# Tail and second half of an attention layer: denominators by transposes, a third weight buffer, residuals loaded ahead, other filler portions

## The chip, the cores and the metric

The kernel runs on one core of one Trainium2 chip, in one launch. The metric is the device time of an execution in microseconds, and the lower it is the better. The engines are TensorE (PE: matrix products and transposes), VectorE (DVE), ScalarE (ACT) and GpSimd (POOL). SyncE (SP) issues nearly all the DMA transfers, in one queue, in order.

## The reference

Two trunk layers over 1024 tokens of width 1024, with 256 context tokens ahead of them. Layer 0 is a mix of chunked gating and Fourier mixing; the change leaves it alone. Layer 1 is windowed attention with 16 query heads, 4 key/value heads of width 64, 256 context keys, a window of 128 to either side, a sink logit for each head and a SiLU gate, then an output product, a gated residual and the final RMS norm over channels:

```
q, k, v, g = split_c(h @ w_in)
...
p = sink_softmax(jnp.concatenate([s_ctx, s_win], axis=-1), sink_b)
...
y = (o * jax.nn.silu(g)) @ w_out_c[i]
...
x = x + gate * y
return rms_norm(x, final_g)
```

So a value after attention is `o` divided by its softmax denominator, times `silu(g)`; that product, called y below, is what the last weight matrix multiplies.

## The kernel before

**Precision and tiles.** Activations stand transposed, channels on partitions and tokens in the free dimension. Every large product is done as three products of split operands: an operand is cast to a short format (hi, by ACT), the rest is subtracted (lo, by POOL or DVE), and hi·hi, lo·hi and hi·lo are accumulated (L108, L109, L110). A 128x1024 weight block comes by DMA into one of three raw buffers (`w_dma`), becomes `wh` on ACT and `wl` on POOL (`w_split`), and serves a tile of 128 output channels. y is split in pieces of 128 channels, k = 0 to 7 (`y_split` puts them in a queue, `pop_y` does one, `need_y` does what a product is about to read).

**The attention.** `attention` runs 32 units: 8 blocks n of 128 queries, with 4 key/value groups j each. `period` is a table of times for one unit u and the next unit v, written by hand and sorted: the score products S of v in two halves (PE, L1626 and L1627), `ttr` (mask and running maximum, DVE, L1644), `exp` (ACT, L1652), transposes T of the probabilities (PE, L1674, into the PSUM tile pt with two buffers), their splits `ph` (ACT) and `pl` (DVE), the products with V of u (PV), and `oev`/`oadd`, which bring the result into `osum`. S of the second half overwrites the scores that `ttr` reads, so it waits for DVE. PE, DVE, ACT and POOL run what the program says in that order; in SP's queue a scheduler has placed the transfers.

**The filler.** Between these steps `F` gives PE other work in portions of PE time, `NF` us for each period: first the products for the gates g and the last q of later blocks (`gen_q`, `gen_g`), then the output product (`gen_out`). That one needs y of the first 512 tokens (c = 0) and so starts in period `SPLIT`, at its tenth us; c = 1 covers tokens 512 to 767. `gen_out` loads the residual `xr` of a tile when it starts it, and its evacuation (DVE, L1492) adds it.

**The denominators.** For a block, `block_a` writes the reciprocals `rinv` to DRAM as `rd`, `block_r` reads them back spread over partitions as `rb`, `block_m` multiplies them with G (`silu(g)`) on POOL and `block_b` multiplies by `osum`. For blocks 0 to 6 that is done once for all 16 heads; for block 7 after each of its 4 units, with 4 heads each.

**The tail.** `tail` does the last 256 tokens in 8 tiles, in the order 6, 7, 0 to 5, with two more pairs of weight buffers (`whx`, `wlx`), and beside it the generator `final` norms what is finished: a column sum on PE, a root on ACT, a reciprocal, a diagonal matrix `t` of it (DVE, L1322), its spread by PE (S<-t,ones, L1329) and the scaled output `ot`. These lines are those that the change alters:

```
def w_dma(self):
    while len(self.raws) < 2 and self.wsrc:
...
if self.raws and len(self.wready) < (2 if self.WT else 1) and (self.WT or self.wn < 31):
...
NF = (4.95, 4.8)
SPLIT = 18
```

## Time and profile before

| | us |
|---|---|
| median of 3 runs | 1116.36 (1116.27 to 1117.07) |
| the profiled execution | 1113.16 |
| its span, first to last instruction | 1111.4 |
| PE busy in it | 1042.1 (94%) |
| DVE, ACT, POOL busy | 660.0, 511.9, 456.2 |
| mean granted clock of PE | 0.977 |

The profiled execution is 3.2 us shorter than the median of the timed runs, and its span is 1.8 us shorter than itself. PE is busy nearly all the time, so what is of interest are the stretches in which it isn't, and those in which its granted clock is below 1.00. The attention starts at 654 us, unit by unit, with a period of 11.7 to 12.3 us where there is filler. Its last product ends at 1052.6 us, the last tile of the tail at 1100.8 us.

### The profile page before, as it was taken

Reading aid. Unit: us, or ns where it says so; the run is one execution under the profiler, and the core shown is the slowest. Engines: PE = TensorE matmul, PEld = TensorE weight load, DVE = VectorE, ACT = ScalarE, POOL = GpSimd, SP = SyncE. Lnnn points to the kernel's source line nnn. Section 1 sums busy time; section 2 is a strip of 40 time slices with the busy share of each in tenths; the row PEclk is TensorE's granted clock in tenths of the full one; section 3 lists DMA queues with packets and bytes.
Section 4 is the critical chain, followed back from the end, with each engine's and each line's share of the span. In section 5 each row is a group of like instructions: output and inputs, shape, how many; then the busy total and the mean of one; then the engine's idle time right before and its main releaser. Section 6 shows DMA issues by size and latency. Waiting matters only on the chain. (4 is left out here: it accounts for less than half of the span.)

```text
span 1111.4 us, 15531 instructions
## 1 busy us (share of the span) xinstructions
PE 1042.1 (94%) x5682; PEld 882.9 (79%) x5682; DVE 660.0 (59%) x1266; ACT 511.9 (46%) x1006; POOL 456.2 (41%) x295
## 2 busy tenths in 40 slices
PE   9889999999999999998989989999999799997885
PEld 7668888887888888886779878888888678886784
DVE  7982666676774545339653006777666767665444
ACT  4463232232122343324232336677666766676642
POOL 2633322253321373547732434666131352436642
PEclk9989999999999999999999999999999999999987
DMA  9720322352124464424421243848242443434344
GB/s 339 269 96 13 120 87 84 109 169 95 57 76 136 148 210 150 140 89 128 146 87 39 95 128 123 131 146 153 58 133 55 109 113 96 99 88 110 105 134 161
DMA packets 102849, 133.94 MB, mean 121 GB/s; under 512 B 24050, under 2 KB 70386, under 8 KB 102772
## 3 DMA queue, kind: packets, MB, share of 16 engines
q1 hardware_dynamic: 101476, 129.13, 39.5%
q0 software_dynamic: 1296, 3.81, 1.1%
q8 instruction: 45, 0.74, 0.3%
q14 instruction: 32, 0.26, 0.1%
HBM read 116.46 MB, written 16.84 MB: 120 GB/s over the span
## 5 line engine op out<-in xcount | busy, mean ns | idle before, releaser
L103 POOL TENSOR_TENSOR wl<-raw,wh 128x1024 fp32r<-128x1024 f32 x80 | 197.9, 2475 | 338.2 <-ACT wh L98 338.2
L110 PE MATMUL mm<-hh,wl 128*128 128x512 f32 (+1 forms) x592 | 215.5, 364 | 3.9 <-POOL wl L103 3.9
L108 PE MATMUL mm<-hh,wh 128*128 128x512 f32 (+1 forms) x592 | 216.8, 366 | 1.4 <-ACT wh L98 1.3
L109 PE MATMUL mm<-hl,wh 128*128 128x512 f32 (+1 forms) x592 | 215.1, 363 | 0.0
L1644 DVE CUSTOM_DVE_ANT_0 P<-S,mask,nsink 128x640 f32<-128x640 f32 (+1 forms) x128 | 103.9, 847 | 90.1 <-PE S L1627 90.1
L1683 DVE TENSOR_TENSOR pl<-pt,ph 128x512 fp32r<-128x512 f32 x152 | 104.0, 689 | 73.1 <-ACT ph L1679 71.3
L110 PEld LDWEIGHTS mm<-hh,wl 128*128 128x128 f32 x592 | 112.1, 189 | 24.2 <-POOL wl L103 4.8
L1679 ACT CAST ph<-pt 128x512 fp32r<-128x512 f32 x152 | 88.4, 584 | 88.1 <-PE pt L1674 87.5
L108 PEld LDWEIGHTS mm<-hh,wh 128*128 128x128 f32 x592 | 112.3, 190 | 20.6 <-ACT wh L98 2.2
L109 PEld LDWEIGHTS mm<-hl,wh 128*128 128x128 f32 x592 | 112.5, 190 | 18.4
L1652 ACT ACTIVATE P<-P,m 128x640 f32<-128x640 f32 (+1 forms) x128 | 101.9, 800 | 7.7 <-DVE m L1644 7.7
L348 DVE CUSTOM_DVE_ANT_0 junk<-raw,cb 128x1024 bf16<-128x1024 f32 x56 | 84.0, 1501 | 27.9 <-DMA raw<-in_ada_wT_dram 27.5
L98 ACT CAST wh<-raw 128x1024 fp32r<-128x1024 f32 x80 | 83.3, 1043 | 28.5 <-PE mm L109 8.9
L1674 PE MATMUL pt<-ident,P 128*128 128x128 f32 x608 | 92.9, 274 | 2.7 <-DVE pl L1683 1.7
L1674 PEld LDWEIGHTS pt<-ident,P 128*128 128x128 f32 x608 | 75.8, 141 | 23.8 <-DVE pl L1683 2.5
L1626 PE MATMUL S<-kk,qh 128*128 128x256 f32 (+1 forms) x256 | 75.0, 310 | 7.4 <-DVE m L1644 5.2
L1627 PE MATMUL S<-kk,ql 128*128 128x256 f32 (+1 forms) x256 | 71.4, 304 | 0.7 <-DMA ql<-qd 0.7
L110 PE MATMUL mm<-rh,hl 128*128 128x512 f32 x160 | 64.3, 402 | 4.5 <-POOL hl L472 4.5
L108 PE MATMUL mm<-rh,hh 128*128 128x512 f32 x160 | 64.8, 405 | 3.6 <-ACT hh L470 3.6
L1691 PE MATMUL O<-ph,V 128*128 128x512 f32 x152 | 63.9, 420 | 1.2 <-DVE osum L1707 0.9
L109 PE MATMUL mm<-rl,hh 128*128 128x512 f32 x160 | 63.4, 396 | 0.0
L1692 PE MATMUL O<-pl,V 128*128 128x512 f32 x152 | 60.8, 400 | 0.3 <-DVE pl L1683 0.3
(270 smaller groups left out, 2203.6 us busy)
## 6 DMA issues: line engine op xcount, KB each, us to landing
raw<-in_w2i_dram SPq DMA_DIRECT2D x34, 512.0 KB, 3.5
raw<-in_ada_wT_dram SPq DMA_DIRECT2D x32, 512.0 KB, 3.5
raw<-in_w2o_dram SPq DMA_DIRECT2D x22, 512.0 KB, 4.0
raw<-in_w1o_dram SPq DMA_DIRECT2D x16, 512.0 KB, 3.5
qh<-qd SPq DMA_DIRECT2D x64, 128.0 KB, 3.9
ql<-qd SPq DMA_DIRECT2D x64, 128.0 KB, 3.7
raw<-in_w1i_dram SPq DMA_DIRECT2D x12, 512.0 KB, 4.7
qd<-t SPq DMA_DIRECT2D x24, 256.0 KB, 4.5
```

The lines of the kernel that those rows point to most:

```text
L98: nc.scalar.copy(out=hi, in_=src)
L103: (nc.vector if lo_eng == "dve" else nc.gpsimd).tensor_tensor(out=lo, in0=src, in1=f32(hi), op=ALU.subtract)
L108: mm(ps, lhsT=lhi, rhs=rhi, start=first, stop=False)
L109: mm(ps, lhsT=lhi, rhs=rlo, start=False, stop=False)
L110: mm(ps, lhsT=llo, rhs=rhi, start=False, stop=last)
L348: nc.vector.tensor_tensor_reduce(out=junk, in0=raw, in1=self.cb[:, i, :], scale=1.0, scalar=0.0, op0=ALU.mult, op1=ALU.add, accum_out=cols ...
L1626: nc.tensor.matmul(S[:, o_:o_ + nn], lhsT=self.qh[:, hs], rhs=kk[:, t0:t0 + nn], start=True, stop=False)
L1644: nc.vector.tensor_tensor_reduce(out=self.P[pr][:, e, :T], in0=k.S[:, so:so + T], in1=k.mask[:, m], scale=-1.0, scalar=k.nsink[:, h:h + 1] ...
L1652: self.K.nc.scalar.activation(out=P, in_=P, func=AF.Exp, bias=self.m[:, h:h + 1], scale=-1.0, accum_out=self.m[:, 16 + h:17 + h])
L1674: nc.tensor.transpose(pt[:, h * 128:(h + 1) * 128], self.P[h // 2][:, h % 2, co:co + 128], k.ident)
L1679: k.nc.scalar.copy(out=self.hl[ci][0], in_=self.pt[ci])
L1683: self.K.nc.vector.tensor_tensor(out=lo, in0=self.pt.pop(ci), in1=f32(hi), op=ALU.subtract)
```

## The change

- `w_dma` of the attention's first weights stands behind the first two units' q loads in the program.
- `NF` is 4.45 and then 4.5, and in the blocks 0 and 7 1.3 more; `SPLIT` is 17.
- `w_split` may run two weights ahead in the attention too, with a third pair of buffers (`wh3`, `wl3`, for every third weight).
- The lo part of y of k = 1, 4 and 7 goes to DVE (in the last 256 tokens, k = 6 and 7 as before).
- `xr` is loaded a tile ahead (`xr_next`), through to the end of the tail.
- Blocks 0 to 6: `block_r` is at 10.0 of the period rather than 2.0, `block_m` at 5.0 rather than 3.0, `block_b` at 8.0 rather than 7.5.
- Block 7: the way through DRAM is gone. `block_t` transposes each head's `rinv`, spread over 128 columns, on PE into a pt buffer, and two DVE instructions multiply G by it; `block_b` multiplies by `osum`.
- Tail: the queued pieces of y go ahead of the first weight split, which the second follows behind the load of ACT's root table; 8 buffers `ot` rather than 4; `t` is made by ACT, but for the last; two more steps lie between it and its use.

```diff
-        self.w_dma()
         for u in U[:2]:
             u.load()
+        self.w_dma()
...
-            nf = self.NF[i >= self.SPLIT]
+            nf = self.NF[i >= self.SPLIT] + (1.3 if u.n in (0, 7) else 0)
...
-    NF = (4.95, 4.8)
-    SPLIT = 18
+    NF = (4.45, 4.5)
+    SPLIT = 17
...
-        for _ in range(2):
-            self.w_split()
+        while self.sq2:
+            self.pop_y()
+        self.w_split()
         dum = self.t(self.const, [128, 1], F32, "dum")
         nc.scalar.activation(out=dum, in_=self.eps, func=AF.Sqrt)
+        self.w_split()
...
-            xr = self.t(self.OP, [128, 512], F32, "xr", 2)
-            nc.sync.dma_start(out=xr[:, hs], in_=self.x1d[:, j, 768:1024])
+            xr = self.xr.pop(0)
+            self.xr_next()
...
-            nc.vector.tensor_scalar(out=dg[:, b * 128:b * 128 + 128], in0=self.ident, scalar1=r[:, b:b + 1],
-                                    scalar2=None, op0=ALU.mult)
-        yield 1
-        yield 1
+            if last:
+                nc.vector.tensor_scalar(out=dg[:, b * 128:b * 128 + 128], in0=self.ident, scalar1=r[:, b:b + 1],
+                                        scalar2=None, op0=ALU.mult)
+            else:
+                nc.scalar.mul(out=dg[:, b * 128:b * 128 + 128], in_=self.ident, mul=r[:, b:b + 1])
+        for _ in range(4):
+            yield 1
...
-                ot = self.t(self.WT, [128, 512], F32, "ot", 4)
+                ot = self.t(self.WT, [128, 512], F32, "ot", 8)
...
-        if self.raws and len(self.wready) < (2 if self.WT else 1) and (self.WT or self.wn < 31):
+        if self.raws and len(self.wready) < 2 and (self.WT or self.wn < 31):
...
-            pool, tg = (self.WT, "x") if self.wn >= 31 else (self.WS, "")
+            pool, tg, nb = (self.WT, "x", 2) if self.wn >= 31 else (self.AT, "3", 1) if self.wn % 3 == 1 else (self.WS, "", 2)
...
-                    lo_eng="dve" if c and hs.start and k > 5 else "pool")))
+                    lo_eng="dve" if (k > 5 if hs.start else k % 3 == 1) else "pool")))
...
+    def xr_next(self):
+        if self.xrl:
+            j, o, hs = self.xrl.pop(0)
+            xr = self.t(self.OP, [128, 512], F32, "xr", 2)
+            self.nc.sync.dma_start(out=xr[:, hs], in_=self.x1d[:, j, o + hs.start:o + hs.stop])
+            self.xr.append(xr)
...
-                at(10.8, self.block_a, v.n, v.j)
+                if v.n < 7:
+                    at(10.8, self.block_a, v.n)
         if u.n == 7 or u.j == 3:
-            at(2.0, self.block_r, u.n, u.j)
+            at(*(1.95, self.block_t, u.j) if u.n == 7 else (10.0, self.block_r, u.n))
         if u.n == 7:
-            at(8.0, self.block_m, u.n, u.j)
             at(10.95, self.block_b, u.n, u.j)
         if prev and prev.n < 7 and prev.j == 3:
-            at(3.0, self.block_m, prev.n, prev.j)
-            at(7.5, self.block_b, prev.n, prev.j)
+            at(5.0, self.block_m, prev.n)
+            at(8.0, self.block_b, prev.n, prev.j)
...
+    def block_t(self, j):
 
         nc = self.nc
...
+        p = self.t(self.ps, [128, 512], F32, "pt", 2)
+        for h in range(4):
+            nc.tensor.transpose(p[:, h * 128:h * 128 + 128], self.bl[7][0][:, 4 * j + h:4 * j + h + 1].broadcast_to([128, 128]), self.ident)
         for e in range(2):
...
+            g = self.G[64 * e:64 * e + 64, 2 * j:2 * j + 2, 896:1024]
+            nc.vector.tensor_tensor(out=g, in0=p[64 * e:64 * e + 64].rearrange("p (i e q) -> p e i q", i=2, e=2)[:, e], in1=g, op=ALU.mult)
```

**Where the order moves.** SP's queue, in before, from the write of block 6's reciprocals (rd6) through that of the first unit of block 7 (rd7); qh and ql are q loads of units to come, raw a weight block:

```order
L1572 DMA rd6_681_4138<-rinv_1459_8363 128x16x1 [waits DMAHW0_49,DVE_49]
L1474 DMA xr_1606_9005<-x1d_537_3179 128x256 [waits DMAHW1_49,DVE_49]
L1584 DMA rb_1579_8903<-rd6_681_4138 64x8x128 [waits DMAHW2_49,DMAHW0_49]
L1584 DMA rb_1579_8903<-rd6_681_4138 64x8x128 [waits DMAHW3_49]
L1382 DMA raw0_1613_9034<-in_w2o_dram 128x1024 [waits DMAHW4_49,Pool_49]
L1617 DMA qh_1616_9043<-qd_674_4131 64x4x128 [waits DMAHW5_49,PE_49]
L1617 DMA qh_1616_9043<-qd_674_4131 64x4x128 [waits DMAHW6_49]
L1617 DMA ql_1617_9044<-qd_674_4131 64x4x128 [waits DMAHW7_49,PE_49]
L1617 DMA ql_1617_9044<-qd_674_4131 64x4x128
L1572 DMA rd7_682_4139<-rinv_1572_8885 128x4x1 [waits DMAHW1_49,DVE_49]
L1474 DMA xr_1627_9124<-x1d_537_3179 128x256 [waits DMAHW2_49,DVE_49]
L1584 DMA rb7_1619_9054<-rd7_682_4139 64x2x128 [waits DMAHW3_49,DMAHW1_49]
```

SP's queue in the changed kernel, from the same write on:

```order
L1584 DMA rd6_681_4138<-rinv_1469_8399 128x16x1 [waits DMAHW2_49,DVE_49]
L1471 DMA xr_1553_8809<-x1d_537_3179 128x256 [waits DMAHW3_49,DVE_49]
L1590 DMA rb_1610_9017<-rd6_681_4138 64x8x128 [waits DMAHW4_49,DMAHW2_49]
L1590 DMA rb_1610_9017<-rd6_681_4138 64x8x128 [waits DMAHW5_49]
L1635 DMA qh_1620_9073<-qd_674_4131 64x4x128 [waits DMAHW6_49,PE_49]
L1635 DMA qh_1620_9073<-qd_674_4131 64x4x128 [waits DMAHW7_49]
L1635 DMA ql_1621_9074<-qd_674_4131 64x4x128 [waits DMAHW0_49,PE_49]
L1635 DMA ql_1621_9074<-qd_674_4131 64x4x128 [waits DMAHW1_49]
L1471 DMA xr_1603_8983<-x1d_537_3179 128x256 [waits DVE_49]
L1387 DMA raw2_1634_9155<-in_w2o_dram 128x1024 [waits DMAHW3_49,Pool_49]
L1635 DMA qh_1650_9247<-qd_674_4131 64x4x128 [waits DMAHW4_49,PE_49]
L1635 DMA qh_1650_9247<-qd_674_4131 64x4x128 [waits DMAHW5_49]
```

The read rb of block 6 still stands directly behind its write and the residual, and q loads behind it; the writes and reads of block 7 are gone, and a weight block and the next residual stand in their place.

POOL in before, from the start of c = 1 (oacc is the sum of squares, wl a weight's lo part, yl a piece of y):

```order
L1500 TENSOR_TENSOR oacc0_1312_7702<-oacc0_1312_7702,t_1567_8873 128x512 [waits Activation_49,Pool_49]
L103 TENSOR_TENSOR wl_1569_8877<-raw0_1513_8618,wh_1568_8876 128x1024 [waits DMAHW6_49,PE_49,Activation_49]
L103 TENSOR_TENSOR yl0_1562_8851<-G_759_4580,yh0_1561_8850 128x256 [waits Activation_49]
L103 TENSOR_TENSOR yl1_1564_8856<-G_759_4580,yh1_1563_8855 128x256 [waits PE_49,Activation_49]
L1500 TENSOR_TENSOR oacc0_1312_7702<-oacc0_1312_7702,t_1610_9027 128x512 [waits Activation_49,Pool_49]
L103 TENSOR_TENSOR wl_1612_9031<-raw1_1539_8744,wh_1611_9030 128x1024 [waits DMAHW5_49,PE_49,Activation_49]
L103 TENSOR_TENSOR yl2_1581_8910<-G_759_4580,yh2_1580_8909 128x256 [waits Activation_49]
L103 TENSOR_TENSOR yl3_1587_8939<-G_759_4580,yh3_1586_8938 128x256 [waits Activation_49]
L1589 TENSOR_TENSOR rb_1579_8903<-rb_1579_8903,G_759_4580 128x1024 [waits DMAHW3_49,DMAHW2_49]
```

POOL in the changed kernel, at the same place:

```order
L103 TENSOR_TENSOR wl_1560_8826<-raw1_1497_8523,wh_1559_8825 128x1024 [waits DMAHW4_49,PE_49,Activation_49]
L103 TENSOR_TENSOR yl0_1556_8816<-G_759_4580,yh0_1555_8815 128x256 [waits PE_49,Activation_49]
L1515 TENSOR_TENSOR oacc0_1295_7616<-oacc0_1295_7616,t_1580_8904 128x512 [waits Activation_49,Pool_49]
L103 TENSOR_TENSOR yl2_1567_8848<-G_759_4580,yh2_1566_8847 128x256 [waits PE_49,Activation_49]
L103 TENSOR_TENSOR yl3_1575_8882<-G_759_4580,yh3_1574_8881 128x256 [waits PE_49,Activation_49]
L103 TENSOR_TENSOR yl5_1590_8932<-G_759_4580,yh5_1589_8931 128x256 [waits PE_49,Activation_49]
L1515 TENSOR_TENSOR oacc0_1295_7616<-oacc0_1295_7616,t_1614_9057 128x512 [waits Activation_49,Pool_49]
L103 TENSOR_TENSOR wl3_1616_9061<-raw2_1533_8705,wh3_1615_9060 128x1024 [waits DMAHW2_49,PE_49,Activation_49]
L103 TENSOR_TENSOR yl6_1596_8961<-G_759_4580,yh6_1595_8960 128x256 [waits Activation_49]
L1595 TENSOR_TENSOR rb_1610_9017<-rb_1610_9017,G_759_4580 128x1024 [waits DMAHW5_49,DMAHW4_49]
```

The last oacc of c = 0 and a weight's lo part still stand together ahead of a piece of y: of yl2 before, of yl6 now, with yl1 and yl4 not on POOL any more.

DVE in before, from the second norm of the tail to the evacuation of the last tile (L1305):

```order
L1287 TENSOR_TENSOR oacc1_1313_7703<-pt_1755_9884,oacc1_1313_7703 128x256 [waits Activation_49]
L1319 RECIPROCAL rl512_1759_9901<-rl512_1759_9901 128x2 [waits Activation_49]
L1322 TENSOR_SCALAR t_1760_9910<-ident_5_100,rl512_1759_9901 128x128 [waits DVE_49,Pool_49]
L1322 TENSOR_SCALAR t_1760_9910<-ident_5_100,rl512_1759_9901 128x128
L1280 SCALAR_TENSOR_TENSOR G_759_4580<-mm_1754_9876,gth_838_5357,xr_1753_9874 128x256 [waits DMAHW4_49,PE_49]
L1287 TENSOR_TENSOR oacc1_1313_7703<-pt_1763_9929,oacc1_1313_7703 128x256 [waits Activation_49]
L1347 TENSOR_TENSOR ot512_1764_9941<-G_759_4580,S_1713_9645 128x256 [waits PE_49]
L1347 TENSOR_TENSOR ot512_1764_9941<-G_759_4580,S_1713_9645 128x256 x2
L1280 SCALAR_TENSOR_TENSOR G_759_4580<-mm_1762_9921,gth_838_5357,xr_1761_9919 128x256 [waits DMAHW0_49,PE_49]
L1287 TENSOR_TENSOR oacc1_1313_7703<-pt_1767_9968,oacc1_1313_7703 128x256 [waits Activation_49]
L1347 TENSOR_TENSOR ot512_1764_9941<-G_759_4580,S_1713_9645 128x256 x5
L1305 SCALAR_TENSOR_TENSOR G_759_4580<-mm_1766_9960,gth_838_5357,xr_1765_9958 128x256 [waits DMAHW1_49,PE_49]
```

DVE in the changed kernel, to the evacuation of the last tile (L1307) and beyond:

```order
L1282 SCALAR_TENSOR_TENSOR G_759_4580<-mm_1757_9886,gth_838_5357,xr_1747_9836 128x256 [waits DMAHW6_49,PE_49,Pool_49]
L1289 TENSOR_TENSOR oacc1_1296_7617<-pt_1766_9938,oacc1_1296_7617 128x256 [waits Activation_49]
L1321 RECIPROCAL rl512_1763_9926<-rl512_1763_9926 128x2
L1282 SCALAR_TENSOR_TENSOR G_759_4580<-mm_1765_9930,gth_838_5357,xr_1756_9884 128x256 [waits DMAHW3_49,PE_49,Pool_49]
L1289 TENSOR_TENSOR oacc1_1296_7617<-pt_1769_9972,oacc1_1296_7617 128x256 [waits Activation_49]
L1352 TENSOR_TENSOR ot512_1770_9984<-G_759_4580,S_1717_9658 128x256 [waits PE_49]
L1352 TENSOR_TENSOR ot512_1770_9984<-G_759_4580,S_1717_9658 128x256 x7
L1307 SCALAR_TENSOR_TENSOR G_759_4580<-mm_1768_9964,gth_838_5357,xr_1764_9928 128x256 [waits DMAHW5_49,PE_49,Pool_49]
L1311 TENSOR_SCALAR G_759_4580<-G_759_4580,fg_673_4129 128x256 [waits Activation_49]
```

The diagonal t of the second norm is not on DVE any more, and all eight outputs ot512 now stand in one piece directly ahead of the evacuation of the last tile, where three of them stood a tile earlier.

## Rows read from the trace of the kernel before

**Rows 1.** Waits of TensorE's (PE) instructions, 650 to 665 us: total us, times, longest.
```profile
PE S L1626 <- DMA qh<-qd: 2.1, 1, 2.1
PE S L1627 <- DMA ql<-qd: 0.7, 1, 0.7
```

**Rows 2.** Stretches, without and with filler: us, busy us per engine (instructions), PEclk, DMA, GB/s.
```profile
860.00:892.00 32.00, 25.87 (x149) 20.34 (x148) 24.22 (x48) 23.89 (x54) 10.98 (x7) 1.00 0.42 109
904.00:1000.00 96.00, 96.00 (x544) 81.34 (x545) 65.37 (x136) 66.14 (x142) 35.36 (x19) 1.00 0.44 112
```

**Rows 3.** Waits of PE's instructions, 785 to 905 us.
```profile
PE S L1626 <- DVE m L1644: 4.0, 7, 1.1
```

**Rows 4.** Waits of PE's instructions, 997 to 1035 us.
```profile
PE mm L110 <- POOL wl L103: 3.4, 2, 1.9
PE mm L109 <- POOL yl L103: 3.1, 2, 2.6
```

**Rows 5.** Waits of PE's instructions, 1035 to 1065 us.
```profile
PE mm L108 <- DVE G L1492: 4.1, 3, 3.1
```

**Rows 6.** Waits of PE's instructions, 1065 us to the end.
```profile
PE S L1329 <- DVE t L1322: 4.3, 2, 3.4
PE mm L109 <- DVE yl L103: 1.9, 1, 1.9
PE mm L108 <- DVE G L1280: 1.4, 1, 1.4
PE mm L108 <- ACT yh L98: 1.0, 1, 1.0
```

**Rows 7.** Stretches from 997.5 us on, columns as in rows 2.
```profile
997.50:1010.00 12.50, 9.45 (x54) 8.25 (x53) 6.25 (x14) 7.23 (x17) 8.94 (x8) 0.86 0.57 138
1022.50:1035.00 12.50, 10.58 (x70) 9.92 (x70) 5.95 (x17) 7.96 (x19) 5.57 (x6) 0.86 0.39 105
1047.50:1060.00 12.50, 9.40 (x64) 8.85 (x63) 2.79 (x6) 4.80 (x10) 6.81 (x6) 0.90 0.26 64
1060.00:1072.50 12.50, 9.36 (x67) 8.75 (x66) 5.02 (x7) 6.80 (x13) 7.84 (x7) 0.91 0.53 180
1072.50:1085.00 12.50, 12.07 (x93) 11.85 (x93) 6.92 (x16) 5.74 (x9) 5.14 (x3) 0.92 0.39 123
1085.00:1097.50 12.50, 7.71 (x45) 7.33 (x44) 7.08 (x13) 2.88 (x6) 4.41 (x2) 0.77 0.52 180
```

**Rows 8.** Chain that ended last, in order of time: start us, us, what.
```profile
996.29 0.23 PE mm L108
...
997.68 0.44 PE pt L1674 x4
...
1044.32 11.63 DMA rd<-rinv
...
1081.11 4.54 DMA out_dram<-ot
```

**Rows 9.** Waits of SP's DMA queue, whole span.
```profile
SPq L1584 <- DMA rd<-rinv: 103.2, 11, 10.4
```

**Rows 10.** Groups on DVE, POOL, ACT, 1000 us on: xcount | busy, mean ns | idle before.
```profile
L1707 DVE TENSOR_TENSOR osum<-O,osum 64x256 f32<-64x256 f32 x10 | 4.2, 417 | 0.1
L1595 DVE TENSOR_TENSOR G<-rb,osum 128x256 f32<-128x256 f32 x4 | 2.9, 714 | 4.1 <-POOL rb L1589 4.0
L1322 DVE TENSOR_SCALAR t<-ident,rl 128x128 f32<-128x128 f32 x8 | 3.6, 501 | 0.2
L1347 DVE TENSOR_TENSOR ot<-G,S 128x256 f32<-128x256 f32 x14 | 4.9, 412 | 1.0 <-ACT rlast L1332 1.0
...
L103 POOL TENSOR_TENSOR wlx<-raw,whx 128x1024 fp32r<-128x1024 f32 x6 | 14.2, 2381 | 14.5 <-ACT whx L98 14.5
...
L98 ACT CAST whx<-raw 128x1024 fp32r<-128x1024 f32 x6 | 6.2, 1041 | 4.9 <-PE mm L109 4.9
```

**Rows 11.** One tile, yl: its DVE instructions, ns min/median/max.
```profile
L103 DVE TENSOR_TENSOR yl<-G,yh x2: 413/1336/2260, 1067.1 to 1069.3; 128x256 fp32r<-128x256 f32 x2
```

More of the change, by code (lines that the diff above doesn't have):

```diff
@@ L1461, in need_y @@
             self.pop_y()
+    def xr_next(self):
[4 more added lines that the diff above has]
+            self.xr.append(xr)
     def gen_out(self):
         self.wkeep = {}
+        self.xrl = [(j, 512 * c, slice(0, 256 if c else 512)) for c in range(2) for j in range(8)]
+        self.xrl += [(j, 512, slice(256, 512)) for j in (6, 7, 0, 1, 2, 3, 4, 5)]
+        self.xr = []
+        self.xr_next()
         for c in range(2):
@@ L1472, in gen_out @@
                     self.wkeep[j] = w
-                xr = self.t(self.OP, [128, 512], F32, "xr", 2)
-                self.nc.sync.dma_start(out=xr[:, hs], in_=self.x1d[:, j, o:o + n])
+                xr = self.xr.pop(0)
+                self.xr_next()
                 p = self.t(self.ps, [128, 512], F32, "mm", self.MMB)
@@ L1565, in period, with block_a @@
         return ev
-    def block_a(self, n, j):
-        nc = self.nc
-        j0, nj = (j, 1) if n == 7 else (0, 4)
-        rinv = self.bl[n][0]
-        nc.sync.dma_start(out=self.rd[n][4 * j0:4 * (j0 + nj)].rearrange("h q -> q h"), in_=rinv[:, 4 * j0:4 * (j0 + nj)],
-                          allow_slow_non_contiguous=True)
-    def block_r(self, n, j):
-        nc = self.nc
-        j0, nj = (j, 1) if n == 7 else (0, 4)
-        if j0 == 0:
-            self.rbs[n] = self.t(self.AT, [128, 8, 128], F32, "rb7" if n == 7 else "rb", 1)
-        rv = self.rd[n].rearrange("(i e) q -> e i q", e=2)
-        s = slice(2 * j0, 2 * (j0 + nj))
-        rb = self.rbs[n][:, s, :]
+    def block_a(self, n):
+        self.nc.sync.dma_start(out=self.rd[n].rearrange("h q -> q h"), in_=self.bl[n][0], allow_slow_non_contiguous=True)
@@ new lines, in block_r, with block_m @@
+    def block_r(self, n):
+        rb = self.rbs[n] = self.t(self.AT, [128, 8, 128], F32, "rb", 1)
+        rv = self.rd[n].rearrange("(i e) q -> e i q", e=2)
+        for e in range(2):
+            self.nc.sync.dma_start(out=rb[64 * e:64 * e + 64], in_=rv[e:e + 1].broadcast_to([64, 8, 128]))
+    def block_m(self, n):
+        rb = self.rbs[n]
+        self.nc.gpsimd.tensor_tensor(out=rb, in0=rb, in1=self.G[:, :, n * 128:(n + 1) * 128], op=ALU.mult)
+    def block_t(self, j):
+        nc = self.nc
+        p = self.t(self.ps, [128, 512], F32, "pt", 2)
+        for h in range(4):
+            nc.tensor.transpose(p[:, h * 128:h * 128 + 128], self.bl[7][0][:, 4 * j + h:4 * j + h + 1].broadcast_to([128, 128]), self.ident)
@@ L1583, in block_r, with block_b @@
         for e in range(2):
-            nc.sync.dma_start(out=rb[64 * e:64 * e + 64], in_=rv[e:e + 1, s, :].broadcast_to([64, 2 * nj, 128]))
-    def block_m(self, n, j):
+            g = self.G[64 * e:64 * e + 64, 2 * j:2 * j + 2, 896:1024]
+            nc.vector.tensor_tensor(out=g, in0=p[64 * e:64 * e + 64].rearrange("p (i e q) -> p e i q", i=2, e=2)[:, e], in1=g, op=ALU.mult)
+    def block_b(self, n, j):
         s = slice(2 * j, 2 * j + 2) if n == 7 else slice(0, 8)
-        rb = self.rbs[n][:, s, :]
-        self.nc.gpsimd.tensor_tensor(out=rb, in0=rb, in1=self.G[:, s, n * 128:(n + 1) * 128], op=ALU.mult)
@@ L1591, in block_b @@
-    def block_b(self, n, j):
+        g, o = self.G[:, s, n * 128:(n + 1) * 128], self.bl[n][1][:, s, :]
         if n == 7:
             self.done7.add(j)
-        s = slice(2 * j, 2 * j + 2) if n == 7 else slice(0, 8)
-        (self.nc.vector if n == 7 else self.nc.gpsimd).tensor_tensor(out=self.G[:, s, n * 128:(n + 1) * 128], in0=self.rbs[n][:, s, :],
-                                     in1=self.bl[n][1][:, s, :], op=ALU.mult)
+            self.nc.vector.tensor_tensor(out=g, in0=g, in1=o, op=ALU.mult)
+        else:
+            self.nc.gpsimd.tensor_tensor(out=g, in0=self.rbs[n], in1=o, op=ALU.mult)
```

3 lines of the change are left out of this document (1 added, 2 removed).

## The prediction

> **What bounds the kernel now.** I read first where TensorE waits, then its clock, then the chain of waits, and last the durations. TensorE is the bound wherever there is filler: from 904 to 1000 us it is busy for 96.00 of 96.00 us at a clock of 1.00 [rows 2]. What this change can win lies in the places where TensorE waits, and all but the first stand from 860 us on:
> - the attention's start: 2.1 and 0.7 us for q loads [rows 1];
> - 860 to 892 us, where the gate products are used up and the output product hasn't begun: 25.87 us busy of 32, so 6.1 idle [rows 2], part of them waits of the scores for DVE's maximum [rows 3];
> - the start of c = 1: 3.1 us for lo parts of y on POOL, then 3.4 us for lo parts of weights [rows 4];
> - from 1035 us: 4.1 us, in 3 waits, for an evacuation on DVE [rows 5]. The chain shows what held it: SP issues in order, the write of four heads' reciprocals takes 11.63 us [rows 8], its read waits for that, and the residual stands behind;
> - the tail: 1.9 and 1.0 us for the last pieces of y, 1.4 us behind an evacuation, 4.3 us in 2 waits for the diagonal t [rows 6].
>
> The clock falls with them. It stands at 0.86 from 997.5, 0.86 from 1022.5, 0.90, 0.91, 0.92 and 0.77 after 1047.5, 1060, 1072.5 and 1085 [rows 7], an average of the levels 2.4 and 1.2 GHz in each stretch. TensorE has waited in or just before each of these stretches, and from 904 to 1000, without a wait, it is at 1.00 [rows 2]. The loss is about (1 - clock) times 12.5 us: 1.75, 1.75, 1.25, 1.1, 1.0 and 2.9, together 9.75 us.
>
> **The change, part by part**, against the profiled execution of 1113.16 us (span 1111.4); the median of the runs is 1116.36, 3.2 higher, and the same difference is then taken off the median.
>
> *Start.* The first weight loads move behind the q loads in the program, but SP's queue, which a scheduler sets, has the raw blocks ahead of q in both kernels. I give it 0; at best the 2.9 us of [rows 1] go.
>
> *Filler.* What `gen_q` and `gen_g` hold for the 17 first periods is about 80 us (all 384 products of 0.23 us [rows 8] are 88.7, less the 9.0 that the head of the attention draws). At 4.95 it is used up after 16.1 periods, and until period 18's tenth us some 2.3 periods run without. Four periods of 5.75 and thirteen of 4.45 make 80.85, so it lasts through period 16, and only period 17 is bare until its tenth us, some 0.8 of a period. 6.1 us for 2.3 periods is 2.65 each, so 2.2 remain: **-3.9**. The price is less cover in each filled period: 0.5 us of products less between steps. The scores already wait for DVE in some filled periods, as part of the 4.0 us of [rows 3]. At most 0.1 us of cover goes ahead of the second half of the scores (0.26 of 0.5), in some 20 periods, so 0 to 2 us; I take **+1**.
>
> *Third weight buffer.* Weights 1 and 2 of c = 1 waited 3.4 us because a split needed the buffer of the tile in work, and came after it: ACT 1.04 and POOL 2.38 us [rows 10] against a tile of 24 products of 256 columns, each half of the 0.23 us of 512 [rows 8], 2.8 us. One weight earlier hides that: **-3.4**. What it doesn't mend is the first wait there, 3.1 us for y [rows 4]: POOL still has the last sum of squares and a weight's lo part ahead of a piece of y, now yl6 rather than yl2. TensorE reads it some 1.4 us later in the tile, but the other pieces are also split as they are needed. I take 0, with bounds of -4.9 (wait and clock gone) and +1.
>
> *Block 7 by transposes.* SP loses four writes of about 10 us and eight reads, and so the residuals, which are also asked for a tile earlier, come in time: **-4.1** [rows 5]. Added are 16 transposes on TensorE, 4 for 0.44 us [rows 8]: **+1.8**, all on the path. DVE gets eight products of 64x256 from PSUM and SBUF, the kind of `oadd` at 0.42 [rows 10], 0.84 for each unit; they stand between the two `ttr` of the first half, and what waits behind is `exp`, and the second half of the scores on TensorE. TensorE has the PV products and filler there, and I let them hide it; without that cover it is 4 x 0.84 = 3.4 us. For the blocks 0 to 6 the read was to be asked later, but SP still has it directly behind its write. SP waits 103.2 us for such writes in all, in 11 waits [rows 9]; the part of blocks 0 to 6 stays, and since 904 to 1000 us has no wait of TensorE it costs nothing there.
>
> *Tail.* After the last PV only `oadd`, `block_b`, a cast and a lo part lie before the last pieces of y: 0.83 + 0.71 + 0.4 + 0.41 [rows 10, 11], some 2.5 us with ACT's copies left out, and 12 products of k = 0 to 5 of tiles 6 and 7 (36 x 0.117 = 4.2 us) cover them. The waits of 1.9 and 1.0 go: **-2.9**. With eight ot buffers DVE doesn't wait for the 4.54 us of an output's write [rows 8], and the 1.4 us behind it go: **-1.4**. Of the 4.3 us for t [rows 6] 3.4 are one wait: two multiplications took over 2 us while POOL split a weight. On ACT, with two more steps to its use, that goes; the other 0.9 belong to the last norm, which stays on DVE: **-3.4**. New: with nothing else late, a weight of the tail is. ACT 1.04, POOL 2.38 and the handing over are some 3.6 us against a tile of 2.8, with norm products between: I take 0.4 for each of 4 weights, **+1.7**. And eight ot512 at 0.35 to 0.41 us [rows 10] now stand ahead of the last evacuation on DVE, 2.9 us where five stood: **+0.8**.
>
> *Clock.* The stretches of [rows 7] after 1022.5 lost 8.0 us, and their long waits are the ones that go. Some short ones come, so I take **-6.3**; the 1.75 before stay.
>
> Gains 3.9 + 3.4 + 4.1 + 2.9 + 1.4 + 3.4 + 6.3 = 25.4; costs 1 + 1.8 + 1.7 + 0.8 = 5.3. Net -20.1: 1093.1 for an execution like the profiled one, **1096.3** for the median.
>
> **A rule that speaks against the change.** The DVE lo part of y shows two durations for one shape, 413 and 2260 ns [rows 11]: the longer ran beside POOL's split of a weight, of 2381 [rows 10]. The Trainium skill, "SBUF — State Buffer", section "SBUF: two separate sides", says that DVE and GpSimd share a pair of ports under an exclusive lock: a DVE instruction with two SBUF inputs and a GpSimd one that reads SBUF run one after the other. By that rule, the trace agreeing here, the product in `block_b` and each y piece moved to DVE can be held for a whole weight split, while `block_t`, with one input from PSUM, isn't; by the rule's worst case the sum would end at the time of the fifth case below, and without the rule at the forecast.
>
> **The rivals.**
> 1. *Everything late is covered.* The start of c = 1 loses its 3.1 and 1.75 us, the tail's weights 1.7, the rest of the clock 1.7. Then 1096.3 - 8.3 = **1088**. For it: a third weight buffer and the pieces of y on two engines. Against: the order on POOL.
> 2. *The tail stays bound by weights and the clock with it.* 0.8 us more on each of 4 weights (3.2), 3 us of clock not won, and half of the 3.4 us of DVE in block 7. Then 1096.3 + 7.9 = **1104**. For it: 3.6 us of split against 2.8 of tile. Against: waits of about a microsecond left the clock at 1.00 from 860 to 892 us [rows 2].
> 3. *The filler doesn't do what is said.* The hole only spreads over the filled periods, in which ACT and DVE set the length: the 3.9 us aren't won, and the cover costs its 2. Then **1101**. For it: the scores' waits in [rows 3].
> 4. *Slower.* The residuals, now asked a tile ahead, wait in SP's queue for a buffer that an evacuation on DVE frees, and q loads stand behind them; from the output product on, 14 periods. It decides if such a wait outlasts the lead of the q loads, about one period less their landing. Then the scores wait as at the start, 2.9 us [rows 1] each; with eight such periods the gain is used up, with ten the time is 1096.3 + 29 = **1125**. Against: the evacuation of a tile ends long before the next but one begins.
> 5. *DVE held by POOL.* Six pieces of y and four `block_b` at 2.26 rather than 0.41 us [rows 11], all exposed: 10 x 1.85 = 18.5 at worst. POOL is busy for 35.36 of 96 us [rows 2], so 37% of them would meet it: 7 us. Then 1096 + 7 = **1103**, and 1115 at worst.
>
> **How the numbers follow.** The forecast (1092 to 1100) has 0.48, the first rival 0.2, the second 0.13, the third 0.07, the fifth 0.06, the fourth 0.06. The range holds the first, the forecast, the third and the second: 1087 to 1106. A measurement of this kernel can tell some 0.2%, or 2.2 us, from no change. Slower has most of the fourth case, 0.05; 0.02 of the fourth and fifth end within 0.2%; faster has the rest, 0.93.
>
> **What would show it.** Right: TensorE's waits for wl from 1000 us on, for G on L1507 and for t are gone or below 0.5 us, its clock is above 0.97 in all stretches from 1022 to 1095 us, one bare period is left before the output product, and 2.9 us at the start and a wait for yl6 after 1000 us remain. Wrong: new waits of the scores for DVE in block 7, waits for wlx above 1 us in the tail, a clock that is still below 0.9 there, or waits for q in the periods with residuals.

## The result, and the profile after

The changed kernel takes 1096.56 us (median of 4 runs, 1096.0 to 1097.5) against 1116.32 of before: a ratio of 0.9823, 95% interval 0.9806 to 0.984, so 19.8 us less. Its profiled execution took 1096.0 us, its span is 1094.1 us, with a mean clock of 0.983. Against the span of before, 1111.4, that is 17.3 us: the traced execution of before was itself 3.2 us below its median, and the one of after only 0.6.

Waits of TensorE in the changed kernel, in the stretches 640 to 670, 670 to 785, 785 to 905, 997 to 1035, 1035 to 1055 and 1055 us to the end (total us, times, longest; the smaller waits of the middle stretches are left out):

```profile
PE S L1644 <- DMA qh<-qd: 2.0, 1, 2.0
PE S L1645 <- DMA ql<-qd: 0.8, 1, 0.8
...
PE O L1709 <- DVE osum L1725: 3.0, 1, 3.0
...
PE S L1644 <- DVE m L1662: 4.4, 6, 2.5
...
PE mm L109 <- POOL yl L103: 2.8, 2, 2.4
PE O L1709 <- DVE osum L1725: 1.7, 1, 1.7
...
PE pt L1602 <- DVE pl L1701: 0.8, 2, 0.5
PE O L1709 <- DVE osum L1725: 0.6, 1, 0.6
...
PE O L1313 <- ACT t L1310: 1.2, 1, 1.2
PE mm L110 <- POOL wlx L103: 1.0, 2, 0.6
PE S L1334 <- DVE t L1325: 0.9, 1, 0.9
```

The two waits for q at the start are as they were in [rows 1]. Of [rows 4] the waits for wl are gone and the one for yl is there still. [rows 5], three waits for an evacuation behind a late residual, has no counterpart. Of [rows 6] the waits for the last y, for ot and for the first t are gone; what is left is 1.0 us for wlx and the last norm. New are waits for `osum` on DVE in block 7 and 3.0 us near 716 us, where before had 1.2:

```profile
PE S L1626 <- DVE m L1644: 1.2, 1, 1.2
```

Stretches of the changed kernel (us, busy us and instructions of PE, PEld, DVE, ACT and POOL, PEclk, DMA share, GB/s):

```profile
860.00:892.00 32.00, 27.80 (x161) 23.18 (x161) 22.97 (x47) 24.97 (x53) 15.89 (x9) 1.00 0.47 124
904.00:1000.00 96.00, 94.18 (x530) 77.98 (x528) 65.00 (x136) 64.74 (x140) 32.18 (x17) 1.00 0.48 110
712.50:725.00 12.50, 9.45 (x47) 8.11 (x46) 6.58 (x15) 4.64 (x10) 7.90 (x5) 0.86 0.86 190
872.50:885.00 12.50, 9.22 (x54) 7.77 (x55) 9.82 (x21) 10.70 (x22) 5.53 (x5) 1.00 0.16 42
997.50:1010.00 12.50, 8.62 (x57) 6.91 (x56) 8.08 (x17) 7.83 (x20) 7.13 (x7) 1.00 0.52 102
1010.00:1022.50 12.50, 11.47 (x80) 10.96 (x78) 6.29 (x13) 6.44 (x16) 6.61 (x3) 0.87 0.40 131
1022.50:1035.00 12.50, 11.57 (x88) 10.76 (x89) 8.80 (x22) 9.91 (x23) 7.43 (x6) 1.00 0.22 69
...
1060.00:1072.50 12.50, 12.23 (x104) 11.93 (x102) 5.56 (x12) 9.58 (x20) 9.53 (x4) 1.00 0.52 158
1072.50:1085.00 12.50, 10.56 (x86) 10.21 (x86) 9.01 (x22) 5.61 (x13) 4.84 (x3) 1.00 0.73 262
```

TensorE is idle for 4.2 us of the 32 from 860 on rather than 6.1, and for 1.8 us of the 96 from 904 on rather than none [rows 2]. The clock is below 1.00 in two of the stretches, 0.86 from 712.5 and 0.87 from 1010 us, each in or just behind a long wait; those that follow up to 1085 us are at 1.00, where [rows 7] had 0.86 to 0.92. From 1085 us on, with 1.24 us of TensorE's work left, it is 0.50.

The start of c = 1 on POOL, and the multiplication that comes 10 us later:

```profile
1005.02 1.30 POOL L1515 TENSOR_TENSOR oacc<-oacc,t 128x512 f32<-128x512 f32 x1 [0.81 <-ACT t L1514]
1006.27 2.36 POOL L103 TENSOR_TENSOR wl<-raw,wh 128x1024 fp32r<-128x1024 f32 x1
1008.58 0.92 POOL L103 TENSOR_TENSOR yl<-G,yh 128x256 fp32r<-128x256 f32 x1
...
1019.25 2.41 POOL L1614 TENSOR_TENSOR G<-rb,osum 128x1024 f32<-128x1024 f32 x1
```

A sum of squares, a weight split and yl6 follow each other, as the order of the changed kernel said; TensorE waits 2.4 us for the last. Beside the multiplication at 1019.25, this is what DVE does:

```profile
1019.59 2.08 DVE L1683 TENSOR_TENSOR es<-es,m 128x4 f32<-128x4 f32 x1
```

An addition of 128x4 numbers (to the denominators, `es`) takes 2.08 us, and the evacuation and `oadd` behind it come late: TensorE's 1.7 us for osum. The chain that ended last, at the tail's end (start us, us, what):

```profile
1076.02 1.04 ACT whx L98
1077.13 2.40 POOL wlx L103
...
1081.53 1.99 DVE ot L1352 x6
```

ScalarE casts the weight, POOL splits it in 2.40 us, TensorE waits 0.6; and the outputs ot512 stand ahead of the last evacuation. The chain runs through six of them, 1.99 us; all eight take 2.74.

### The profile page after: what moved, and what is told of

The parts are those of the page before. It is cut to its first block, busy times and chain, and to the rows that moved or that the text cites. A ratio compares the mean times of both kernels' runs of the same rounds, so it can differ in the third digit from the quotient of the medians.

```text
span 1094.1 us, 15534 instructions
## 1 busy us (share of the span) xinstructions
PE 1036.7 (95%) x5698; PEld 877.8 (80%) x5698; DVE 666.2 (61%) x1274; ACT 513.9 (47%) x1012; POOL 447.2 (41%) x285
## 4 chain that ended last, share of the span: by engine, by line
PE 63%; DVE 18%; DMA 7%; ACT 5%; issue 4%; POOL 3%; SPq 0%; DVEq 0%; ACTq 0%; POOLq 0%
PE mm L108 12%; PE mm L110 12%; PE mm L109 12%; DVE junk L348 6%; PE mm L1156 6%; PE pt L1692 4%; DMA raw<-in_ada_wT_dram 3%; PE S L1644 3%; PE S L1645 3%; PE O L1710 2%; PE O L1709 2%; DVE P L1662 1%; DMA qd<-rx 1%; DVE pl L1701 1%; DVE y L658 1%
## 5 line engine op out<-in xcount | busy, mean ns | idle before, releaser
L108 PEld LDWEIGHTS mm<-hh,wh 128*128 128x128 f32 x592 | 112.2, 189 | 20.1 <-ACT wh L98 1.7
L1644 PEld LDWEIGHTS S<-kk,qh 128*128 128x128 f32 x256 | 49.0, 191 | 15.8 <-DVE m L1662 11.5
```

What stands on the lines that cost most here:

```text
L108: mm(ps, lhsT=lhi, rhs=rhi, start=first, stop=False)
L1644: nc.tensor.matmul(S[:, o_:o_ + nn], lhsT=self.qh[:, hs], rhs=kk[:, t0:t0 + nn], start=True, stop=False)
```

## The experiments

The kernel before was run beside each and took 1119.1 to 1122.1 us there, so kernels are compared by their ratio to it: 0.9823 for the changed kernel. A step of 0.001 is 1.1 us. The changed kernel's own ratio is from the runs of the result; two kernels below that differ from it by one small edit, u_xr and u_yl, came out at 0.9823 and 0.9826. Costs below are given to the microsecond; the intervals are some 3 to 6 us to either side.

**Taking a part back out of the changed kernel.** First the transposes (u_dram7):

```diff
-            at(*(1.95, self.block_t, u.j) if u.n == 7 else (10.0, self.block_r, u.n))
+            at(*(2.0, self.block_r7, u.j) if u.n == 7 else (10.0, self.block_r, u.n))
...
+            at(8.0, self.block_m7, u.j)
```

> The changed kernel with block 7's reciprocals sent through DRAM again (write, read, GpSimd multiply, per unit); all else as changed. Theory: SyncE is held for about 11 us by each of four writes, so residuals and weights come late again, though now asked a tile ahead, and the last pieces of y wait for the last write: the last unit's chain gives 11.6 + 2.6 + 0.7 us behind its denominators, against some 7 us of products left, so a wait of TensorE of 5 to 9 us around 1055 us and a clock below 0.9 there; the transposes' 1.8 us and the waits for DVE's osum in block 7 (1.7 and 0.6 us) go. Net 5 to 12 us slower than the changed kernel, 1102 to 1109. Rival: the residuals asked a tile ahead hide the writes by themselves, and without the 1.8 us of transposes and the waits in block 7 it is as fast or up to 3 us faster, 1093 to 1097.

1113.36 us, ratio 0.9924 (0.9896 to 0.9953), some 11 us slower than the changed kernel. Its TensorE from 1000 us on:

```profile
PE mm L109 <- POOL yl L103: 9.4, 3, 6.2
PE S L1660 <- DVE m L1678: 4.9, 3, 3.1
PE O L1726 <- DVE pl L1717: 2.2, 1, 2.2
```

The last pieces of y come 6.2 us late, as expected. No wait of TensorE for an evacuation stands there, but the residuals are late all the same, and DVE waits for them, 4.8 us for one that was issued directly behind a write:

```profile
DVE G L1507 <- DMA xr<-x1d: 6.8, 3, 4.8
```

In before DVE waited 6.0 us for them in two. DVE, whose `block_b` waits for the reads (10.0 us) as well, now holds the scores (4.9 us) and a PV product (2.2 us). The rival is out.

The third weight buffer (u_third):

> The changed kernel with two weight buffers in the attention again. Theory: waits of TensorE for wl return at the first tiles of c = 1 (3.4 us in before) with a clock of about 0.86 in one stretch (1.75 us): 3.5 to 5.5 us slower, about 1101. Rival: with the residuals in time and transposes between, tiles take longer than a split, the waits stay under 1 us, and it is within 1 us.

```diff
-        if self.raws and len(self.wready) < 2 and (self.WT or self.wn < 31):
+        if self.raws and len(self.wready) < (2 if self.WT else 1) and (self.WT or self.wn < 31):
```

1109.94 us, 0.9897 (0.9851 to 0.9944), some 8 us slower:

```profile
PE mm L110 <- POOL wl L103: 8.1, 6, 1.9
```

Six waits for weights and 8.1 us, where before had two and 3.4 [rows 4]. Neither theory had the size. Transposes and two buffers by themselves don't make the weights so late: with the transposes put into before (a_t7, below) the waits are 2.8 us. Among what still differs between the two kernels is the portion in block 7, 5.8 us here and 4.8 there, some two tiles of 2.8 us in each period; but the prefetch, the pieces of y on DVE and the period at which the output product starts differ too. That the portion is the cause is argued, and wasn't run by itself.

The tail (u_tail):

> The changed kernel with the tail of before (two splits ahead of the last pieces of y, all diagonals t on DVE, two steps to their use, four ot buffers); residuals still a tile ahead. Theory: the waits of 1.4 us (ot) and 3.4 us (t, DVE held while GpSimd splits a weight) return, and with them the clock of 0.77 in one stretch (2.9 us); the last pieces of y on DVE stand beside two weight splits and take over 2 us again, 1 to 2 us of wait. 7 to 10 us slower, 1103 to 1107. Rival: with the last block in time the norms come at other points of the tail, and t and ot are not late: under 3 us slower.

```diff
-        while self.sq2:
-            self.pop_y()
-        self.w_split()
+        for _ in range(2):
+            self.w_split()
...
-            if last:
+            if True:
...
-        for _ in range(4):
+        for _ in range(2):
...
-                ot = self.t(self.WT, [128, 512], F32, "ot", 8)
+                ot = self.t(self.WT, [128, 512], F32, "ot", 4)
```

1112.16 us, 0.9924 (0.9899 to 0.9949), some 11 us slower:

```profile
PE S L1332 <- DVE t L1323: 4.3, 2, 3.4
PE mm L109 <- DVE yl L103: 1.9, 1, 1.9
PE mm L108 <- DVE G L1280: 1.6, 1, 1.6
```

The wait for t, that for ot and that for the last lo parts of y stand there again, 3.4, 1.6 and 1.9 us; the clock is 0.79 from 1060 and 0.86 from 1085 us. The rival, by which the norms would no longer be late, is out.

The filler (u_fill):

> The changed kernel with the filler portions and the start of the output product of before (4.95 and 4.8 us, from period 18). Theory: the hole without filler is 2.3 periods long again (6.1 us of TensorE idle from 860 to 892 us in before, 4.3 us from 870 to 885 in the changed one), the waits of 0.2 to 0.3 us of the scores from 905 to 1000 us go (1.4 us together), and the 3.05 us at 716 us, where the q products of block 0 were ahead of their stores, fall back to about 1.2. Net about 0 to +2 us against the changed kernel. Rival, as forecast: 3 us or more slower.

```diff
-            nf = self.NF[i >= self.SPLIT] + (1.3 if u.n in (0, 7) else 0)
+            nf = self.NF[i >= self.SPLIT]
...
-    NF = (4.45, 4.5)
-    SPLIT = 17
+    NF = (4.95, 4.8)
+    SPLIT = 18
```

1099.21 us, 0.9806 (0.9761 to 0.9851): by the ratio nothing that can be told from the changed kernel. Waits of the scores from 785 to 910 us:

```profile
PE S L1644 <- DVE m L1662: 4.7, 7, 1.7
```

They sum to 4.7 us, 4.4 in the changed kernel. The hole is longer here (25.50 us busy in the 32 from 860 us on, 27.80 in the changed kernel), and in the time the two can't be told apart, as the theory had it: 3 us for this part don't show. But the wait near 716 us did not fall back to 1.2 us:

```profile
PE S L1644 <- DVE m L1662: 2.5, 1, 2.5
```

The clock from 712.5 us is 0.86 here as well. In the three kernels with the changed portions that ran beside this one (u_dram7, u_third, u_tail) the wait is 4.7 to 4.8 us; the two kernels made from before (a_t7, a_tail), with before's portions, have 2.3. So the portions do lengthen it, by some 2 us, but the 1.2 us of the traced execution of before are the least of all, and old portions don't keep the clock up.

The residuals (u_xr):

> The changed kernel with each residual asked when its tile starts, as in before. Theory: with block 7's writes gone from SyncE's queue, residuals land in 5 us within a tile's time, and only the one behind block 6's write is late: within 1 us of the changed kernel. Rival: the prefetch itself took away the 4.1 us, then waits of TensorE for the evacuation behind xr return: 3 us or more slower.

```diff
-                xr = self.xr.pop(0)
-                self.xr_next()
+                self.xr_next()
+                xr = self.xr.pop(0)
```

1098.89 us, 0.9823 (0.9788 to 0.9858): no difference, and no wait for an evacuation in the trace. u_dram7, which has the prefetch and the writes, has no such wait of TensorE either. But there DVE still waits 6.8 us for residuals and TensorE waits elsewhere, so of the two edits it is the end of the writes that brings the residuals in time.

The pieces of y on DVE (u_yl):

> The changed kernel with all lo parts of y (but the last two of the last 256 tokens) on GpSimd again. Theory: the wait of 2.5 us of the scores for DVE in the bare period shrinks by about 0.7, since no y piece stands between DVE's two maxima there; at the start of c = 1 eight pieces of y stand on GpSimd behind a sum and a weight split, so the 2.4 us wait grows to 3 or more. Net within 1.5 us of the changed kernel. Rival (DVE held by GpSimd is the price of those pieces): 3 us or more faster.

```diff
-                    lo_eng="dve" if (k > 5 if hs.start else k % 3 == 1) else "pool")))
+                    lo_eng="dve" if hs.start and k > 5 else "pool")))
```

1097.84 us, 0.9826 (0.9771 to 0.9881): no difference, so the pieces on DVE cost nothing that shows, and win nothing. In its trace the bare period's wait is 1.85 us rather than 2.5, as expected, and the waits for yl from 1000 us on are 2.2 us in three, not more than 3.

**One part alone, put into before.** The transposes (a_t7), and then the tail (a_tail):

> The kernel before with one part of the change alone: block 7's reciprocals by transposes rather than through DRAM; residuals asked at their tile, two weight buffers, the old tail and filler. Theory (the parts share one path, so each is worth less alone than its removal from the changed kernel costs, 17 us there): the waits behind the residual (4.1 us) and the last block (1.9 and 1.0 us) go, 1.8 us of transposes come, but tiles that no longer wait for residuals wait for weights instead, four or five times 1 to 2 us: 2 to 6 us faster than before. Rival (terms add): as the removal costs, 12 to 17 us faster.

```diff
-            at(2.0, self.block_r, u.n, u.j)
+            at(*(1.95, self.block_t, u.j) if u.n == 7 else (2.0, self.block_r, u.n, u.j))
...
-            at(8.0, self.block_m, u.n, u.j)
```

1112.78 us, 0.9912 (0.9886 to 0.9939), 9.9 us faster than before; between the theory and its rival. TensorE from 1000 us on:

```profile
PE mm L110 <- POOL wl L103: 2.8, 2, 1.9
PE mm L109 <- DVE yl L103: 1.9, 1, 1.9
PE mm L108 <- DVE G L1492: 0.8, 1, 0.8
```

Of the 4.1 us of [rows 5] 0.8 are left. The last y still takes 1.9 us, since the old tail splits two weights ahead of it.

> The kernel before with the changed tail alone (pieces of y ahead of the second split, eight ot buffers, diagonals on ScalarE, two more steps); residuals of the tail asked at their tile, block 7 through DRAM. Theory: the 3.4 us for t and the 1.4 us for ot are in the tail alone and go, with the clock of 0.77 in the stretch from 1085 us (2.9 us); the last pieces of y still come late with the last reciprocals. 6 to 9 us faster than before. Rival: under 3 us, as weights are late in place of t.

The lines of the tail that `u_tail` takes out, here put into before; two of them:

```diff
-                ot = self.t(self.WT, [128, 512], F32, "ot", 4)
+                ot = self.t(self.WT, [128, 512], F32, "ot", 8)
...
-            nc.vector.tensor_scalar(out=dg[:, b * 128:b * 128 + 128], in0=self.ident, scalar1=r[:, b:b + 1],
-                                    scalar2=None, op0=ALU.mult)
+                nc.scalar.mul(out=dg[:, b * 128:b * 128 + 128], in_=self.ident, mul=r[:, b:b + 1])
```

1113.07 us, 0.9917 (0.9887 to 0.9946), 9.3 us faster than before, just beyond the theory's upper end:

```profile
PE mm L110 <- POOL wl L103: 5.0, 3, 2.8
PE mm L108 <- DVE G L1497: 2.9, 3, 2.0
```

No wait for t of block 0 or for ot is left, but weights (5.0 us, 3.4 in before) and the residual (2.9 us) are still late. What each of the two parts wins alone, 9.9 and 9.3 us, is near the 11 us that its removal costs, with intervals of some 3 us on each.

**What is left in the changed kernel.** First the held addition:

```diff
-            at(8.0, self.block_b, prev.n, prev.j)
+            at(5.05, self.block_b, prev.n, prev.j)
```

> The changed kernel with the last multiplication of blocks 0 to 6 on GpSimd directly behind the first (5.05 rather than 8.0 of the period), so that it does not run beside the sum of the denominators on DVE. Theory: at 1019.6 us an addition of 128x4 numbers took 2.08 us on DVE rather than 0.15, beside that multiplication of 2.41 us; moved, it takes 0.15 to 0.5, TensorE's 1.7 us wait at 1021.5 goes, 1.5 to 2 us faster. Rival: the addition was held by something else (the exponentials on ScalarE), and the wait stays.

1096.19 us, 0.9799 (0.9765 to 0.9833). The addition on DVE in this kernel:

```profile
1021.69 0.15 DVE L1683 TENSOR_TENSOR es<-es,m 128x4 f32<-128x4 f32 x1
```

0.15 us with POOL idle, against 2.08 beside its multiplication, and TensorE's 1.7 us wait is gone. The step in the time, 0.0024, lies within the intervals; the cause of the wait is shown by the traces. Next the 3 us near 716 us:

> The changed kernel with 4.76 us of filler in each period up to 16 rather than 5.75 in block 0 and 4.45 behind it. Theory: the 3.05 us wait of TensorE at 716 us came from block 0's larger portions: a q product's evacuation reached DVE while its buffer t was still to be stored, and the store stood in SyncE's queue behind block 0's reciprocals; with even portions it is 1.2 us or less, as in before, and the scores' waits around 790 to 900 us shrink by some 0.5 us: 2 to 3 us faster. Rival: the wait moves to another period and nothing is won.

```diff
-            nf = self.NF[i >= self.SPLIT] + (1.3 if u.n in (0, 7) else 0)
+            nf = self.NF[i >= self.SPLIT] + (1.3 if u.n == 7 else 0)
...
-    NF = (4.45, 4.5)
+    NF = (4.76, 4.5)
```

1100.19 us, 0.9832 (0.9799 to 0.9865), not faster. The wait near 716 us and a stretch behind the hole:

```profile
PE S L1644 <- DVE m L1662: 2.9, 4, 2.0
...
872.50:885.00 12.50, 8.81 (x43) 7.15 (x43) 8.17 (x17) 9.39 (x20) 4.00 (x4) 0.86 0.16 46
```

It is 2.0 us rather than 3.0 (3.5 to 3.6 in u_xr, u_yl and the kernel with the multiplication moved, which ran beside it), and of the scores for DVE, and the clock fell behind the hole, where it stayed at 1.00 in the changed kernel. The portions change its size, and don't take it away. Is it SyncE, held by the write of block 0's reciprocals? In the changed kernel SyncE issues that write at 702.66, two stores of q at 705.50, and is held until 715.21; DVE stands until 716.06:

```profile
702.66 0.39 SPq L1584 DMA_DIRECT2D rd<-rinv  x1
705.50 1.69 SPq L1042 DMA_DIRECT2D qd<-t  x2
715.21 1.26 SPq L1590 DMA_DIRECT2D rb<-rd  x2
```

```profile
716.06 0.01 DVE L1423 LOAD_MASK_SELECT t<-t  x1 [5.80 <-DMA qd<-t]
```

> The changed kernel with four edits: the second multiplication of blocks 0 to 6 directly behind the first; the first two units' q loads issued by ScalarE; y's lo part of k = 6 of c = 1 on DVE too; the reads of the reciprocals of blocks 0 to 6 issued by GpSimd. Theory: gone are the 1.7 us behind the held addition, the 2.4 us at the start of c = 1 (now some 0.5), the 3 to 4.8 us at 716 us (SyncE no longer waits for a write, so the q products' stores leave at once) with up to 1.75 us of clock each for the last two, and, if ScalarE gets to the q loads before SyncE's weight loads land, 1 to 2.9 us at the start. 5 to 9 us faster than the changed kernel, 1088 to 1092 where that has 1096.6. Rival: GpSimd, which waits for the write in SyncE's place, holds weights and pieces of y, and the gain is under 2 us or a loss.

1107.71 us, 0.9877 (0.9837 to 0.9918), not faster and by the medians some 6 us slower. Two of the four edits, the second the one that was to free SyncE, and what SyncE and DVE then do:

```diff
-            u.load()
+            u.load(nc.scalar)
...
-            self.nc.sync.dma_start(out=rb[64 * e:64 * e + 64], in_=rv[e:e + 1].broadcast_to([64, 8, 128]))
+            self.nc.gpsimd.dma_start(out=rb[64 * e:64 * e + 64], in_=rv[e:e + 1].broadcast_to([64, 8, 128]))
```

```profile
712.65 0.39 SPq L1584 DMA_DIRECT2D rd<-rinv  x1
715.50 1.71 SPq L1042 DMA_DIRECT2D qd<-t  x2
717.84 4.11 SPq L1635 DMA_DIRECT2D qh<-qd  x2
```

```profile
727.74 0.01 DVE L1423 LOAD_MASK_SELECT t<-t  x1 [7.46 <-DMA qd<-t]
```

SyncE goes on to q loads at 717.84, 5 us after the write; DVE waits for the store all the same, 7.46 us, and TensorE 4.7. So my theory of SyncE's hold falls: the stores are issued in time, and it is their landing that is late. ScalarE's q loads at the start and the piece of y on DVE didn't pay either (2.1 us for that piece at the start of c = 1). Nearly half of the loss of the traced execution, 7.6 us of 16.3 against that of the changed kernel, stands ahead of all four edits: its first store of q is issued at 515.1 us rather than 507.5, with a clock of 0.59 from 12.5 to 25 us. Where the rest came from is open: in the attention the clock was at 0.73 to 0.86 in five stretches. What the edits cost is therefore not shown, only that the 5 to 9 us weren't won.

> The changed kernel with block 0's reciprocals by transposes as well, unit by unit like block 7's, so that the first write to DRAM is block 1's, and with the multiplications of blocks 1 to 6 on GpSimd one behind the other. Theory (formed after the reads were moved to GpSimd and the wait of 4.7 us near 720 us stayed): the q products' stores are issued some 3 us behind block 0's write and land only after it, 10.7 us late and more, though SyncE itself is free; DVE waits for them to reuse their buffer. Without that write the wait of 3 to 4.8 us goes, and the clock stays at 1.00 in the stretch from 712 us (up to 1.75 us); 1.8 us of transposes and up to 1 us on DVE come; with 1.6 us for the multiplications: 3 to 5 us faster than the changed kernel. Rival: the stores are late by themselves, the wait stays, and it is within 1 us of the kernel with the multiplications moved alone, or slower by the transposes.

```diff
-            at(*(1.95, self.block_t, u.j) if u.n == 7 else (10.0, self.block_r, u.n))
+            at(*(1.95, self.block_t, u.n, u.j) if u.n in (0, 7) else (10.0, self.block_r, u.n))
...
-            at(8.0, self.block_b, prev.n, prev.j)
+            at(5.05, self.block_b, prev.n, prev.j)
```

1095.42 us, 0.9782 (0.975 to 0.9814), the lowest ratio of all; its interval still touches that of the changed kernel. All waits of TensorE from 670 to 785 us:

```profile
PE S L1646 <- DVE m L1664: 0.2, 1, 0.2
```

Without block 0's write nothing holds TensorE near 716 us, 0.2 us rather than 3.0, and the clock from 712.5 us is 1.00. The stores of q issued at 709.41 land in 2.0 us there, where those of the changed kernel at 705.50 take 10.5; and behind block 1's write, which is left, two more take 10.8. So it is the write that makes them late, and the rival is out. How much time that won isn't shown: the medians, of different sets of runs, differ by 1.1 us, and the ratios by 0.0041, with intervals that overlap.

## Why the prediction was right, point by point

The time, 1096.56, is the forecast's 1096.3, but the agreement is better than the working. Between the two traces it is 17.3 us where the sum was for 20.1. Most terms hold in mechanism and size; four don't: the filler was given too much, block 7 and block 0 cost what the sum put at nothing, and the way in which the residuals came late was misread.

- *Start:* 0 forecast, the waits of 2.0 and 0.8 us are there, as 2.1 and 0.7 were (2.8 together, not the forecast's 2.9). Right: SP's order had not changed.
- *Filler:* -3.9 and +1 forecast. By the busy time, TensorE's idle time from 785 to 904 us fell from 9.1 to 5.9 us, and from 904 to 997 it rose from 0 to 1.4: -1.9 in place of -2.9. The bare period has a wait of 2.5 us, longer than any of the old hole; 0.6 of it is the piece of y on DVE, as u_yl shows. With block 0, below, the portions as a whole won nothing that shows, as u_fill has it.
- *Weights:* -3.4, right; but without the third buffer they wait 8.1 us in the changed kernel, not 3.4. My sum priced the buffer against the waits of before alone.
- *Start of c = 1:* 0 forecast, 2.8 us of waits for yl in place of 3.1, and the clock at 0.87. Right, with the mechanism read off the order.
- *Residuals:* -4.1, right in size, but not in the way. I had the residual stand in SP's queue behind the read that waits for the write. The trace of before has two residuals issued directly behind the write of 1044.32 and ahead of its read at 1055.97, as the order of SP's queue has it too. They landed only 11.1 us later, and DVE, which waited 5.7 us for them, evacuated at 1056.21. The stores of q behind block 0's write meet the same. With block 7's writes gone the wait goes, and u_xr shows that the prefetch isn't needed for it. The issue, and then its KB each and median us to landing:

```profile
1044.79 0.93 SPq L1474 DMA_DIRECT2D xr<-x1d  x2
...
xr<-x1d SPq DMA_DIRECT2D x2, 128.0 KB, 11.1
```

- *Block 7:* +1.8 for transposes, and DVE's products let go as hidden. DVE was late in block 7: 2.3 us of waits for osum, of which before had 0.4, and 1.1 us for its `pl` ahead of the transposes. 1.7 of it is the fifth rival in a place that I hadn't looked at, the sum of denominators beside a multiplication on POOL. The Trainium skill, "SBUF — State Buffer", section "SBUF: two separate sides", has the rule of that lock for a DVE instruction with two SBUF inputs; 2.08 against 0.15 us agrees with it, and the y pieces on DVE, of two shapes, 558 ns in the median here and 939 at most, mostly escaped it.
- *Block 0:* not in the forecast at all. 1.9 us of wait and a clock of 0.86 (1.75 us). The wait comes from stores of q that land late behind the write of the reciprocals, as the kernel without that write shows, and the larger portions lengthen it. That the clock fell through the portions isn't shown: with the old ones u_fill has 0.86 there too, and the kernel with the multiplication moved has 1.00 behind a wait of 3.5 us.
- *Tail:* -2.9, -1.4, -3.4 as forecast; the waits for wlx grew by 0.6 rather than 1.7. All eight ot512 stand ahead of the last evacuation, as forecast, and the wait for the last square is 1.2 us rather than 0.7: +0.5 rather than +0.8.
- *Clock:* -6.3 forecast. By (1 - clock) times 12.5 the stretches after 1022.5 us lost 8.0 us in before and nothing up to 1085 us now. 1.7 us better than the sum.

So the misses, +1.0 for the filler, +3.0 for block 7 and +3.7 for block 0, together 7.7, met 5.2 the other way: the clock (1.7), the tail (1.4), y (0.3) and a clock of 1.00 behind the first wait for q, where before had 0.96 and 0.90 (1.75, and no part of the change). That is 2.5 of the 2.8 us by which the traces fall short of the sum; and the traced execution of before, 3.2 us under its median, where that of the changed kernel was 0.6 under, makes up for them. That all this came out within 0.3 us is luck.

Of the rivals, the first (1088) fails by the start of c = 1, though two of its terms came in good part: the clock after 1022.5 us (1.7) and the tail's weights (1.1 of 1.7). The second fails by a clock of 1.00 in the tail. The third is nearer than its time says: the hole did shrink, but with the cover and block 0 the portions as a whole won nothing that shows. Of the signs, the waits for wl and for G on L1507 are gone and those for q at the start and yl6 remain; 0.9 us for the last norm's t remain, as the sum had it and the sign did not, and the clock is 1.00 only up to 1085 us. DVE in block 7 did come late, for osum and not for the scores.
